# Later output projections one stage earlier, and the second group's operands inside the down-projections

## The chip, the cores and the metric

The kernel runs on one core of a Trainium2 chip. Its times are device microseconds of one launch; the profile adds one execution recorded by the hardware profiler. The engines are TensorE (PE for matmuls, PEld for weight loads), VectorE (DVE), ScalarE (ACT), GpSimd (POOL) and SyncE (SP), whose queue issues the transfers. Each runs its own instructions in a fixed order and waits on semaphores.

## The reference

One decoder layer for 2048 tokens of width 1024, in float32: a normalized and modulated input, attention beside a state-space mixer, an output projection, and a gated feed-forward of width 2816.

```python
mod = silu(c) @ w_ada + b_ada                       # shift1, scale1, gate1, shift2, scale2, gate2
h = modulate(rmsnorm(x, norm1_w), shift1, scale1)
q, k, v, z, xbc, dt_raw = split(h @ w_in)
attn = sliding_window_attention(rope(q), rope(k), v, sinks)      # window 128, 8 heads of 64
y = ssd_chunked_scan(silu(conv(xbc)), softplus(dt_raw), ...)     # chunks of 128, 8 heads of 64
y = grouped_rmsnorm(y * silu(z)) * ssm_norm_w
x = x + gate1 * (concat([attn, y]) @ w_out)
h = modulate(rmsnorm(x, norm2_w), shift2, scale2)
g, u = split(h @ w_gate_up)
x = x + gate2 * ((silu(g) * u) @ w_down)
return rmsnorm(x, final_norm_w)
```

## The kernel before

The 2048 tokens are four blocks of 512 (b = 0 to 3); two blocks make a group (s = 0, 1). Tiles have 128 partitions. Every float32 product is made of three passes (`mm3`, L269 to L271, or L876 to L878 in the feed-forward): each operand is split into a high and a low half, and high x high, high x low and low x high are added in PSUM. The splits are work of ACT (L807: the high half of a weight; L957: of an activation; L247: of a mixer output; L832 and L837: of a feed-forward operand) and of VectorE or GpSimd (L808, L802, L833: the low half). Split weights lie in a ring of six pairs (`w`), loaded weights in a ring of five (`raw`), passing values in a ring of eight (`t`), dense sums in four PSUM banks (`d`).

The stages follow each other on PE:
1. `opening()` (L1022): the modulation vectors (products with `w_ada`, L193 and L1052 on VectorE, and `ada_columns`, L173, through PE), the first norm of block 0, and the rotary tables `rope_tables` (L205, L207 to L223): for the sine and then the cosine, three operations (L214 to L216) round the angle, four (L219 to L222) reduce it, and ACT takes the sine (L223). `ready(d)` makes chunk d of the normalized input (L318, L320, L321); `whole(d)` also its modulation (two L1052). The rotary products are L369 and L370.
2. Input projections of the four blocks (`queries`, `keys_values`, `convolved`, `gated`), with the mixers (`attentions`, `ssds`) beside them.
3. `quads(0)` (L1254): gate and up projections of the first group as 22 `quad`s (L880) of seven half-size products each, in place of eight. Their operands are sums and differences of blocks: `operands_first` (L843), `operands_between` (L851), `operands_last` (L858). These load a block's residual from `mid` (L826), scale it by the root of the norm spread over partitions (L827; `at`, `am` and `bc` are that spread root), and split it into 28 pairs. The mixers of the last blocks run beside `quads(0)`.
4. `down(0)` and `down(1)` (L943): the down projections of blocks 0 and 1, in six groups g of the hidden width (five of four tiles, one of two), each with eight output chunks; L968 adds a PSUM sum to the residual and frees its bank. After a block, `final` writes the output: L997 on VectorE, L998 on SP. Beside them run `out_proj(2)` and `out_proj(3)` (L765; two halves for each of eight output chunks, weights by L257), whose 16 split inputs `mo` are loaded by `mixed` (L759), and the second group's operands.
5. `quads(1)`, `down(2)`, `down(3)`.

What sets the order: "beside" means that a main generator yields after each piece, and `tick(ratio)` adds `ratio` to a counter; whenever it reaches one, the first generator of the list `sides` makes a step. In stages 1 and 2 the instructions of PE (in the opening also of VectorE, SP and ACT) stand in the order in which the program writes them. In the rest a scheduler in the build orders each engine's instructions by its own model of their times. On the chip the orders are fixed.

`quad` also holds its first weight loads back: for the quad named `behind`, they are issued after the last load of `scaled`:

```python
with tc.issue_after(scaled.last.ins) if behind else nullcontext():
    a11, a21, a22, a12 = (load_w(wgu[f, u, half]) for u, half in ((0, 0), (1, 0), (1, 1), (0, 1)))
```

In the kernel before, `sides` beside `down(0)` holds `projections()`: both output projections and, beside the rest of the second, `operands_first` of the second group. Once that is done, within `down(1)`, the projections' pool is closed, the remaining operand tiles take its memory, and the remaining 20 of the 28 pairs are made beside the rest of `down(1)`.

## Time and profile before

| | us |
|---|---|
| median of 3 runs | 2442.17 |
| lowest, highest | 2438.68, 2443.37 |
| the profiled execution's own time | 2445.11 |
| its span | 2443.4 |
| PE busy, POOL busy, DVE busy, ACT busy | 2270.3, 1225.7, 1438.8, 969.1 |
| the first matmul of `down(0)` at | 1335.1 |
| the first matmul of `quads(1)` at | 1717.7 |

The granted clock of PE, averaged over the span, is 0.964. Times in the views count from the span's start. In a row of a timeline the first number is the start, the second the duration; what stands in brackets is the idle time of that engine before, and whose work ended it. PE's matmuls are pipelined, so its busy time is no measure of its peak; its idle pieces are what can be read.

### The profile page before, as it was taken

The page shows a single profiled execution, that of the slowest core. Times are in us where ns is not written, and L with a number is a line of the kernel's source. Part 1 is how long each engine was busy: PE and PEld are TensorE (multiplying, and loading weights), DVE is VectorE, ACT ScalarE, POOL GpSimd, SP SyncE. Part 2 cuts the span into 40 slices and gives each one's busy share as a digit, 9 for nine tenths or more (in the row PEclk, how much of TensorE's full clock was granted, in tenths as well). Part 3 has the DMA queues.
Part 4 walks back from the last instruction along what each step waited for, and adds up shares of the span by engine and source line. Part 5 has one row for each costly group of instructions (what it writes and reads, how often), then busy time and mean ns, then how long its engine had stood idle before and what let it go on. Part 6 is the DMA issues. An engine that isn't in the chain of part 4 may idle for free.

```text
span 2443.4 us, 33147 instructions
## 1 busy us (share of the span) xinstructions
PE 2270.3 (93%) x11304; PEld 1892.1 (77%) x11304; DVE 1438.8 (59%) x2543; ACT 969.1 (40%) x2011; POOL 1225.7 (50%) x1227
## 2 busy tenths in 40 slices
PE   6786999899899799999999999897799999999898
PEld 4676888789788688887887878686688888878687
DVE  5876874665366855576655534648854544444544
ACT  3454452555155545433334323223333333333332
POOL 1765533444124755587775224235766666643431
PEclk9898999999999899999999999899899999999998
DMA  6898978677775322233235665764422222263451
GB/s 243 275 336 282 315 241 260 218 242 241 261 266 173 125 82 73 75 117 96 86 95 183 195 194 163 239 199 143 163 85 76 95 78 78 82 215 104 136 166 52
DMA packets 249065, 412.22 MB, mean 169 GB/s; under 512 B 22464, under 2 KB 68544, under 8 KB 248896
## 3 DMA queue, kind: packets, MB, share of 16 engines
q1 hardware_dynamic: 247744, 409.05, 51.3%
q8 instruction: 89, 1.46, 0.2%
q10 hardware_dynamic: 1152, 1.05, 0.1%
q14 instruction: 80, 0.66, 0.1%
HBM read 315.58 MB, written 94.44 MB: 168 GB/s over the span
## 4 chain that ended last, share of the span: by engine, by line
PE 68%; DVE 11%; DMA 6%; POOL 5%; ACT 4%; issue 4%; SPq 1%; DVEq 0%; ACTq 0%; POOLq 0%
PE d L269 10%; PE d L271 10%; PE d L270 10%; PE d L878 7%; PE d L876 7%; PE d L877 7%; PE am L269 1%; PE am L270 1%; PE am L271 1%; PE am L878 1%; PE am L876 1%; PE am L877 1%; DMA t<-in_xT_dram 1%; DMA t<-mid 1%; DVE w L808 1%
## 5 line engine op out<-in xcount | busy, mean ns | idle before, releaser
L876 PE MATMUL d<-b,w 128*128 128x512 f32 x924 | 368.8, 403 | 31.6 <-ACT w L807 21.4
L807 ACT ACTIVATE w<-raw 128x512 fp32r<-128x512 f32 x316 | 198.2, 630 | 448.0 <-PE d L271 249.5
L878 PE MATMUL d<-b,w 128*128 128x512 f32 x924 | 368.6, 400 | 3.0 <-DVE w L808 3.0
L877 PE MATMUL d<-b,w 128*128 128x512 f32 x924 | 370.6, 401 | 0.6 <-POOL b L838 0.6
L269 PE MATMUL d<-a,w 128*128 128x512 f32 (+1 forms) x720 | 280.5, 399 | 16.1 <-ACT a L957 14.3
L270 PE MATMUL d<-a,w 128*128 128x512 f32 (+1 forms) x720 | 282.7, 394 | 0.1
L271 PE MATMUL d<-a,w 128*128 128x512 f32 (+1 forms) x720 | 282.6, 393 | 0.0
L808 POOL TENSOR_TENSOR w<-raw,w 128x512 fp32r<-128x512 f32 x88 | 119.0, 1353 | 278.7 <-ACT w L807 270.8
L808 DVE TENSOR_TENSOR w<-raw,w 128x512 fp32r<-128x512 f32 x228 | 210.2, 925 | 67.3 <-ACT w L807 65.9
L968 DVE SCALAR_TENSOR_TENSOR x<-d,mod,x 128x512 f32<-128x512 f32 (+1 forms) x182 | 131.1, 725 | 197.7 <-PE d L271 193.0
L876 PEld LDWEIGHTS d<-b,w 128*128 128x128 f32 x924 | 175.8, 190 | 73.2 <-ACT w L807 22.2
L269 PE MATMUL d<-w,hl 128*128 128x256 f32 (+1 forms) x608 | 181.9, 299 | 36.1 <-DVE s L370 16.6
L878 PEld LDWEIGHTS d<-b,w 128*128 128x128 f32 x924 | 175.7, 190 | 42.9 <-DVE w L808 4.2
L877 PEld LDWEIGHTS d<-b,w 128*128 128x128 f32 x924 | 176.1, 191 | 40.4 <-POOL b L838 1.3
L807 ACT ACTIVATE w<-s 128x512 fp32r<-128x512 f32 x176 | 111.0, 632 | 227.1 <-PE d L878 177.0
L808 POOL TENSOR_TENSOR w<-s,w 128x512 fp32r<-128x512 f32 x132 | 186.6, 1415 | 26.1 <-ACT w L807 25.7
L271 PE MATMUL d<-w,hl 128*128 128x256 f32 (+1 forms) x608 | 178.0, 293 | 2.1 <-DVE hl L321 2.1
L270 PE MATMUL d<-w,hl 128*128 128x256 f32 (+1 forms) x608 | 177.6, 292 | 0.0
L269 PEld LDWEIGHTS d<-a,w 128*128 128x128 f32 x720 | 137.4, 191 | 50.6 <-ACT a L957 17.0
L892 POOL TENSOR_TENSOR s<-raw,s 128x512 f32<-128x512 f32 x44 | 58.6, 1332 | 206.8 <-DVE w L808 125.0
L270 PEld LDWEIGHTS d<-a,w 128*128 128x128 f32 x720 | 137.4, 191 | 31.7 <-DVE a L802 1.0
L271 PEld LDWEIGHTS d<-a,w 128*128 128x128 f32 x720 | 137.3, 191 | 31.2
(356 smaller groups left out, 5476.4 us busy)
## 6 DMA issues: line engine op xcount, KB each, us to landing
raw<-in_wgu_dram SPq DMA_DIRECT2D x176, 256.0 KB, 2.8
raw<-in_wd_dram SPq DMA_DIRECT2D x176, 256.0 KB, 2.7
w<-w_x SPq DMA_DIRECT2D x48, 512.0 KB, 5.3
w<-w_o SPq DMA_DIRECT2D x48, 512.0 KB, 4.5
act<-t SPq DMA_DIRECT2D x88, 256.0 KB, 2.1
t<-act SPq DMA_DIRECT2D x88, 256.0 KB, 4.5
t<-in_xT_dram SPq DMA_DIRECT2D x80, 256.0 KB, 4.4
aw<-in_wada_dram SPq DMA_DIRECT2D x64, 256.0 KB, 4.3
```

The lines of the kernel that those rows point to most:

```text
L269: nc.tensor.matmul(out, ahi, bhi, start=first, stop=False)
L270: nc.tensor.matmul(out, ahi, blo, start=False, stop=False)
L271: mm3.last = nc.tensor.matmul(out, alo, bhi, start=False, stop=last)
L807: nc.scalar.activation(hi, x, AF.Copy)
L808: eng.tensor_tensor(lo, x, hi.bitcast(F32), ALU.subtract)
L876: nc.tensor.matmul(out, ahi, bhi, start=first and k == 0, stop=False, skip_group_check=True)
L877: nc.tensor.matmul(out, ahi, blo, start=False, stop=False, skip_group_check=True)
L878: mm3.last = nc.tensor.matmul(out, alo, bhi, start=False, stop=k == 3, skip_group_check=True)
L892: nc.gpsimd.tensor_tensor(s4, a12, s2, ALU.subtract)
L968: nc.vector.scalar_tensor_tensor(x, ps, gate2[:, c:c + 1], x, ALU.mult, ALU.add)
```

## The change

The multiset of instructions on each engine stays; their order changes.

- `RATIO_UP`, the pace of the mixers beside `quads(0)`, goes from 0.6 to 0.64. As soon as they are done, their memory is given back, and in it (a pool `op` on the right side) `first_output()` starts beside the rest of `quads(0)`: the loads of `mo` (a ring of 11 pairs, not 16) and `out_proj(2)`. What of it is left goes on beside `down(0)`.
- Beside `down(0)` follow `second_output()` (`out_proj(3)`) and `first_operands()`, at a pace of 0.55. When `sides` is empty, the pool `op` is closed, the remaining operand tiles take its place, and `last_operands()` (the 20 other pairs) runs beside `down(1)` at 0.3.
- Attention of blocks 1 to 3 waits no step (2 before) before its first tile.
- In the opening the sine's reduction is made before the first chunk (`next(tables)` before `ready(0)`), the cosine's after `ready(7)`, and ACT takes both sines at the end; the second set of modulation columns (`ada_columns`) comes before `whole(5)`.

Lines of the changed kernel stand four below those of the kernel before (L876 is L880, L826 is L830).

VectorE in the opening. Before, from the end of `ready(7)` to the first rotary products (L219 to L222 are the table's reduction, `aw` is `w_ada`):

```order
L219 SCALAR_TENSOR_TENSOR m_243<-m_242,m_240 128x512
L193 ISA aw,part<-aw,csil,vec 128x512
...
L220 SCALAR_TENSOR_TENSOR m_243<-m_242,m_243 128x512
...
L221 SCALAR_TENSOR_TENSOR m_243<-m_242,m_243 128x512
L222 TENSOR_SCALAR m_243<-m_243 128x512
L214 TENSOR_SCALAR m_665<-m_240 128x512
...
L219 SCALAR_TENSOR_TENSOR m_666<-m_665,m_240 128x512
...
L220 SCALAR_TENSOR_TENSOR m_666<-m_665,m_666 128x512
...
L221 SCALAR_TENSOR_TENSOR m_666<-m_665,m_666 128x512
L222 TENSOR_SCALAR m_666<-m_666 128x512
L369 TENSOR_TENSOR m_681<-d,cos 128x8x32
```

Now:

```order
L325 SCALAR_TENSOR_TENSOR hl_611<-t,mod,hl_611 128x512
L215 TENSOR_SCALAR m_664<-m_240 128x512
...
L216 TENSOR_SCALAR m_664<-m_664 128x512
...
L217 TENSOR_SCALAR m_664<-m_664 128x512
L220 SCALAR_TENSOR_TENSOR m_665<-m_664,m_240 128x512
...
L221 SCALAR_TENSOR_TENSOR m_665<-m_664,m_665 128x512
L222 SCALAR_TENSOR_TENSOR m_665<-m_664,m_665 128x512
...
L223 TENSOR_SCALAR m_665<-m_665 128x512
L373 TENSOR_TENSOR m_681<-d,cos 128x8x32
```

Only the cosine's seven operations are left between, and four L193 products in place of six (one L193 row is shown, in the first piece).

ScalarE at the end of the mixers in `quads(0)`. Before (L674 scales the mixer's last transposed output, `a` are the inputs of `down(0)`):

```order
L674 ACTIVATE m_13199<-st,vec 128x128 x4
L807 ACTIVATE w<-raw 128x512
L903 ACTIVATE t<-d 128x512
L907 ACTIVATE t<-d 128x512
L807 ACTIVATE w<-raw 128x512 x4
L930 ACTIVATE t<-t 128x512
L807 ACTIVATE w<-raw 128x512
L957 ACTIVATE a<-t 128x512 x4
L247 ACTIVATE mo<-t 128x512 x6
```

Now:

```order
L748 ACTIVATE m_12933,ss<-m_12866 128x256 x2
L811 ACTIVATE w<-s 128x512 x2
L755 ACTIVATE m_12866<-m_12866,rs 128x256 x2
L811 ACTIVATE w<-s 128x512
L678 ACTIVATE m_12933<-st,vec 128x128 x4
L251 ACTIVATE mo<-t 128x512 x6
L911 ACTIVATE t<-d 128x512
L251 ACTIVATE mo<-t 128x512 x2
```

The splits of `mo`, which stood behind the inputs of `down(0)`, follow the mixer's last scaling at once.

SyncE at the end of `down(1)`. Before:

```order
L826 DMA t<-mid_208 128x512
L813 DMA raw<-in_wd_dram 128x512
L826 DMA t<-mid_208 128x512 x2
L826 DMA t<-mid_207 128x512 x2
...
L813 DMA raw<-in_wgu_dram 128x512 x11
L998 DMA out_dram<-t 128x512
```

(the pair of rows with two loads each from `mid_208` and `mid_207` stands there four times). Now:

```order
L830 DMA t<-mid_208 128x512 x2
L830 DMA t<-mid_207 128x512
L817 DMA raw<-in_wd_dram 128x512
L830 DMA t<-mid_207 128x512
L817 DMA raw<-in_wd_dram 128x512 x2
L959 DMA t<-act_214 128x512 x2
L817 DMA raw<-in_wd_dram 128x512 x3
L817 DMA raw<-in_wgu_dram 128x512 x13
```

The last operand loads are now mixed with the loads of `w_down`, and the first loads of `w_gate_up` for `quads(1)` follow the last of these directly.

```diff
--- before.py
+++ after.py
@@ -29,7 +29,7 @@
 NEG = -1e30
 RAW, SPLIT = 5, 6
 TMP, M1, M2, M4 = 8, 3, 8, 4
-MIX, RATIO_UP = 1.1, 0.6
+MIX, RATIO_UP = 1.1, 0.64
 HALF = 32
 ROPE_THETA = 10000.0
 TWO_PI_1 = 6.25
@@ -209,6 +209,7 @@
         ang3 = ang.rearrange("p (t j) -> p t j", j=HALF)
         nc.vector.tensor_tensor(ang3, posf.unsqueeze(2).broadcast_to([P, S // P, HALF]),
                                 invf.unsqueeze(1).broadcast_to([P, S // P, HALF]), ALU.mult)
+        angles = []
         for dst, turn in ((sin, 0.0), (cos, 0.25)):
             k, r = common.m2(), common.m2()
             nc.vector.tensor_scalar(k, ang, 1.0 / (2 * math.pi), turn, ALU.mult, ALU.add)
@@ -220,6 +221,9 @@
             nc.vector.scalar_tensor_tensor(r, k, -TWO_PI_2, r, ALU.mult, ALU.add)
             nc.vector.scalar_tensor_tensor(r, k, -TWO_PI_3, r, ALU.mult, ALU.add)
             nc.vector.tensor_scalar(r, r, PI_IN, -PI_IN, ALU.min, ALU.max)
+            angles.append((dst, r))
+            yield
+        for dst, r in angles:
             nc.scalar.activation(dst.rearrange("p t j -> p (t j)"), r, AF.Sin)
         yield
 
@@ -535,7 +539,7 @@
             return q, kv
 
         held, nxt = None, load(0)
-        for _ in range(3 if b == 0 else 2):
+        for _ in range(3 if b == 0 else 0):
             yield
         for t in range(NT):
             gt, (q, kv) = b * NT + t, nxt
@@ -1084,6 +1088,7 @@
         ada_products(first, line, range(4, 8))
         reduced(0, rows0[1])
         scale_of(0)
+        next(tables)
         ready(0)
         weights(raws[0])
         main = queries(0, h)
@@ -1099,15 +1104,16 @@
         next(main)
         whole(4, rows4)
         weights(raws[2])
-        whole(5, rows5)
         line = side_bank(0)
         ada_products(second, line, range(8))
+        ada_columns(line, side_bank(0), 6)
+        whole(5, rows5)
         next(main)
-        ada_columns(line, side_bank(0), 6)
         weights(raws[3])
         ready(6)
         ready(7)
         next(main)
+        next(tables)
         drain(tables)
         return h, main
 
@@ -1255,63 +1261,70 @@
         for f in range(NF):
             yield from quad(s, f, ops, banks(f), f == 0, f == behind)
 
-    with tc.tile_pool(name="b0l", bufs=1, reuse_waits="tile") as bp:
-        operand_tiles(ops, bp, ("b22", "t3", "t2", "t4"))
-        main = quads(0, ops, lambda f: [dense() for _ in range(4)], 1)
-        next(main)
-        drain(operands_last(0, ops, bcs))
-        drain(beside(main, RATIO_UP))
-        finish(sides[-1] if sides else None)
+    bp = early.enter_context(tc.tile_pool(name="b0l", bufs=1, reuse_waits="tile"))
+    operand_tiles(ops, bp, ("b22", "t3", "t2", "t4"))
+    main = quads(0, ops, lambda f: [dense() for _ in range(4)], 1)
+    next(main)
+    drain(operands_last(0, ops, bcs))
+    for _ in beside(main, RATIO_UP):
+        if not sides:
+            break
+    finish(sides[-1] if sides else None)
+    mixing.close()
+    outputs = ExitStack()
+    op = outputs.enter_context(tc.tile_pool(name="op", bufs=1, side="right", reuse_waits="tile"))
+    mixes, ops = {2: [], 3: []}, {}
+
+    def output(b, each=lambda c: None):
+        yield from out_proj(b, y_of, mixes[b], lambda c: side_bank(c % 2), sums(op), lambda: side_bank(2), each)
+
+    def loaded(b, c):
+        mixed(b, mixes[b], (c,), lambda c: pair("mo", 11, pool=op))
+
+    def first_output():
+        for c in range(KT):
+            loaded(2, c)
+            if c % 2:
+                yield
+        yield from output(2, lambda c: loaded(3, c - 5) if c > 4 else None)
+
+    def second_output():
+        for c in range(3, KT):
+            loaded(3, c)
+            if c % 2:
+                yield
+        yield from output(3)
+
+    def first_operands():
+        bc = big("bc", 1, pool=op)
+        nc.scalar.copy(bc, spread(y_of[2], bc=side_bank(3)))
+        yield from operands_first(1, ops, [bc])
+
+    def last_operands():
+        bcs = [spread(y_of[2 + j], bc=side_bank(j)) for j in range(2)]
+        yield from operands_between(1, ops, bcs)
+        yield from operands_last(1, ops, bcs)
+
+    sides.append(first_output())
+    drain(beside(main, 0.5))
     early.close()
-    mixing.close()
-    dn = ctx.enter_context(tc.tile_pool(name="dn", bufs=1, side="right", reuse_waits="tile"))
-    with tc.tile_pool(name="b1", bufs=1, reuse_waits="tile") as bp:
-        ops = {}
+    dn = ctx.enter_context(tc.tile_pool(name="dn", bufs=1, reuse_waits="tile"))
+    with tc.tile_pool(name="b1", bufs=1, reuse_waits="tile") as bp, ExitStack() as late:
         operand_tiles(ops, bp, ("b11", "b21"))
-        with tc.tile_pool(name="op", bufs=1, reuse_waits="tile") as op:
-            mixes = {2: [], 3: []}
-
-            def outputs(b, each=lambda c: None):
-                yield from out_proj(b, y_of, mixes[b], lambda c: side_bank(c % 2), sums(op), lambda: side_bank(2), each)
-
-            def loaded(b, c):
-                mixed(b, mixes[b], (c,), lambda c: pair("mo", 16, pool=op))
-
-            def projections():
-                for c in range(KT):
-                    loaded(2, c)
-                    if c % 4 == 3:
-                        yield
-                yield from outputs(2, lambda c: loaded(3, c))
-                rest3 = outputs(3)
-                for _ in range(2):
-                    next(rest3)
-                    yield
-                bc = big("bc", 1, pool=op)
-                nc.scalar.copy(bc, spread(y_of[2], bc=side_bank(3)))
-                yield from both(rest3, operands_first(1, ops, [bc]))
-
-            sides.append(projections())
-            drain(beside(down(0, dn, dn), 0.42))
-            rest = down(1, dn, dn)
-            for _ in beside(rest, 0.8):
-                if not sides:
-                    break
-        with tc.tile_pool(name="b1l", bufs=1, reuse_waits="tile") as bp:
-            operand_tiles(ops, bp, ("t1", "b22", "t3", "t2", "t4"))
-            bcs = [spread(y_of[2 + j], bc=side_bank(j)) for j in range(2)]
-
-            def remaining():
-                yield from operands_between(1, ops, bcs)
-                yield from operands_last(1, ops, bcs)
-
-            sides.append(remaining())
-            last = sides[-1]
-            drain(beside(rest, 0.4))
-            finish(last)
-            for i, _ in enumerate(quads(1, ops, lambda f: [side_bank(i) if f % 2 else dense() for i in range(4)], 0)):
-                if i in (0, 2):
-                    norm_of_block_before(2)
+        sides.extend([second_output(), first_operands()])
+        last = None
+        for b in range(2):
+            for _ in beside(down(b, dn, dn), 0.3 if last else 0.55):
+                if not sides and last is None:
+                    outputs.close()
+                    bp = late.enter_context(tc.tile_pool(name="b1l", bufs=1, reuse_waits="tile"))
+                    operand_tiles(ops, bp, ("t1", "b22", "t3", "t2", "t4"))
+                    last = last_operands()
+                    sides.append(last)
+        finish(last)
+        for i, _ in enumerate(quads(1, ops, lambda f: [side_bank(i) if f % 2 else dense() for i in range(4)], 0)):
+            if i in (0, 2):
+                norm_of_block_before(2)
     drain(down(2, dn, dn))
     x3 = ctx.enter_context(tc.tile_pool(name="x3", bufs=1, reuse_waits="tile"))
     drain(down(3, dn, x3))
```

## The prediction

> **What bounds the kernel now.** I read the page first, then the table of waits of TensorE, then the windows by stage, then the timelines around the four longest waits.

> ```profile
> span 2443.4 us, 33147 instructions
> PE 2270.3 (93%) x11304; PEld 1892.1 (77%) x11304; DVE 1438.8 (59%) x2543; ACT 969.1 (40%) x2011; POOL 1225.7 (50%) x1227
> ```

> PE is busy 93% of the span and no other engine reaches 60%. The change gives every engine the same instructions as before, in another order. So PE's 2270 us can only shrink where they ran at half clock; what can move otherwise is the 173 us in which PE waits. The waits are few and named:

> ```profile
> PE d L876 <- ACT w L807: 21.4, 1, 21.4
> PE d L269 <- DVE s L370: 16.6, 2, 16.3
> PE d L269 <- ACT a L957: 14.3, 6, 3.2
> PE am L269 <- DMA w<-w_o: 8.3, 1, 8.3
> PE d L878 <- DVE w L808: 3.0, 2, 2.5
> PE st L313 <- DVE t L311: 3.9, 2, 2.1
> ```

> The columns are the total, the number of times and the longest. The first, second and fourth rows, 46 us in three waits, all lie where the change works. By stage (us, then busy time of PE, PEld, DVE, ACT, POOL, then PE's granted clock):

> ```profile
> 1335.00:1520.00 185.00, 181.81 (x770) 146.71 (x771) 83.18 (x108) 60.72 (x101) 65.15 (x48) 0.98 0.61 198
> 1520.00:1600.00 80.00, 69.92 (x289) 55.36 (x288) 45.77 (x86) 20.52 (x34) 18.60 (x14) 0.91 0.68 218
> 1600.00:1660.00 60.00, 60.00 (x265) 48.75 (x264) 31.49 (x53) 17.93 (x30) 21.29 (x16) 1.00 0.61 194
> 1660.00:1722.00 62.00, 40.13 (x162) 31.08 (x161) 54.96 (x68) 24.69 (x42) 40.09 (x28) 0.81 0.45 142
> 1722.00:1760.00 38.00, 33.35 (x130) 25.48 (x130) 35.32 (x41) 10.98 (x19) 29.72 (x22) 0.91 0.51 170
> ```

> The first row is most of `down(0)`, the second the hand-over from `down(0)` to `down(1)`, then `down(1)` in two pieces, then the start of `quads(1)`. PE is full in the first and third (60 us hold 265 matmuls, 0.226 us each); in the fourth VectorE is busy 55 of 62 us and PE waits. The work that makes VectorE late there was waiting to start while VectorE idled half of 1335 to 1660. That unevenness is what the change rearranges.

> **The opening** (PE waits 16.3 us for the first rotary products, which need both tables).

> ```profile
> 24.11 0.75 DVE L318 SCALAR_TENSOR_TENSOR t<-m,scl,at 128x512 f32<-128x512 f32 x1 [3.01 <-PE at L313]
> 69.90 0.68 DVE L219 SCALAR_TENSOR_TENSOR m<-m,m 128x512 f32<-128x512 f32 x1
> 81.78 1.75 DVE L193 CUSTOM_DVE_ANT_0 aw<-aw,csil,vec 128x512 f32<-128x512 f32 x1
> 85.12 0.74 DVE L193 CUSTOM_DVE_ANT_0 aw<-aw,csil,part 128x512 f32<-128x512 f32 x1
> 87.56 0.43 DVE L222 TENSOR_SCALAR m<-m 128x512 f32<-128x512 f32 x1
> 88.68 0.42 DVE L369 TENSOR_TENSOR m<-d,cos 128x256 f32<-128x256 f32 x1 [0.70 <-ACT cos L223]
> ```

> After the last normalized chunk VectorE runs eleven table operations and six L193 products from 69.90 to 87.99, 18.1 us, and only then the rotary products. The sine half (four operations: two neighbours of the first and last, 0.68, 0.68, 0.68, 0.43) now fits into an idle piece of 3.0 us that ended at 24.11; two L193 products (1.75 and 0.74) fall behind the rotary products. Removed: 2.5 + 2.5 = 5.0 us. What stays, seven table operations and four products, costs between 7 us (each at its short duration, 0.43, 0.68 or 0.74) and 13.1 us (18.1 less 5.0, with the long ones as they were). So the gain is 5 to 11, nearer 5 since what stretched the products there is not touched; against it stand the column sums of the modulation, which now precede chunk 5 and delay that chunk, covered by key/value matmuls already mixed in. **I take 6.5 us**, ends 3 and 10.

> **The end of `quads(0)`.** The mixers now end about 100 matmuls sooner (`RATIO_UP` 0.64), and eleven of the sixteen half-chunks of `out_proj(2)` fill the tail. Two prices. First, the last mixer's chain on PE, ACT and GpSimd:

> ```profile
> 1297.10 1.03 PE L716 MATMUL st<-state,m 128*128 128x256 f32 x4
> 1312.65 0.91 ACT L751 ACTIVATE m<-m,rs 128x256 f32<-128x256 f32 x2 [1.12 <-POOL rs L238]
> 1317.10 1.14 ACT L674 ACTIVATE m<-st,vec 128x128 f32<-128x128 f32 x4 [0.26 <-PE st L671]
> ```

> From L716 to the end of L751 it took 16.5 us. Before, PE had other work until the transposes L671; now only 55 matmuls (12.5 us at 0.226) stand between, so PE waits about 3 us at the transposes. Then ACT must do the four L674 scalings (1.14 us) and the first splits of `mo` before `out_proj(2)` can start, since they are queued behind those scalings and it follows the transposes at once: about 2 us more. Such a gap also costs clock:

> ```profile
> 1335.00:1339.00 4.00, 3.89 (x12) 0.70 1.02 364
> 1335.11 1.19 PE L269 MATMUL d<-a,w 128*128 128x512 f32 x4 [2.27 <-ACT a L957]
> ```

> The gap of 2.27 us at the start of `down(0)` was followed by a granted clock of 0.70 over 4 us, 1.2 us lost. So **+6 us**, ends 0 (VectorE and GpSimd run the chain uncontended and the splits are early) and 10. [...] Second, the `w_o` loads. They precede their matmuls by 26 to 56 matmuls, 6 to 13 us, and the page has

> ```profile
> w<-w_o SPq DMA_DIRECT2D x48, 512.0 KB, 4.5
> 1549.37 0.84 SPq L257 DMA_DIRECT2D w<-w_o  x1
> 1556.65 0.79 PE L269 MATMUL am<-mo,w 128*128 128x512 f32 x1 [8.27 <-DMA w<-w_o]
> ```

> 4.5 us to landing in the median, against the 7.2 us of the one load (issued at 1549.37, PE released at 1556.6) that held PE for 8.3 us. The tightest would then be 1 us late: nothing taken, end +3. `down(0)` itself loses `out_proj(2)` and keeps a VectorE that is busy 83 of 185 us: nothing.

> **The hand-over.** Row two of the stages: 10.1 us idle, and 80 x 0.09 = 7.2 us of clock, 17.3 us in all. The `w_o` wait goes, since those loads now stand 40 matmuls ahead. What is left is a burst on SP's queue: loads of the residual and of the activations stand behind eight output stores that wait for VectorE's L997, and I read two waits of PE from the order, about 3 and 3.5 us, each with 1.2 of clock: 8.9. **Gain 8 us**, ends 2 and 13.

> **The second group's operands in `down(1)`.** This is the 21.4 us.

> ```profile
> 1674.55 38.83 SPq L826 DMA_DIRECT2D t<-mid  x16
> 1713.72 2.23 SPq L813 DMA_DIRECT2D raw<-in_wgu_dram  x5
> 1717.70 0.79 PE L876 MATMUL d<-b,w 128*128 128x512 f32 x1 [21.36 <-ACT w L807]
> ```

> The releaser named, ACT, is only the last link: SP stood 38.8 us with sixteen loads that waited for buffers that VectorE had to free, the gate and up weights are queued behind them, arrived from 1713.72 on, and PE started 4 us later. In the change all 28 steps of the operands run inside `down(1)` and the weight loads are queued before its end, so this queue is gone. Its price is that 432 matmuls of `down(1)` (98 us at 0.226) now carry 146 VectorE instructions. Their durations in this stretch of the run before:

> ```profile
> L968 DVE SCALAR_TENSOR_TENSOR x<-d,mod,x 128x512 f32<-128x512 f32 x48 | 35.5, 747 | 48.8 <-PE d L271 44.2 <-DMA x<-mid 4.6
> L808 DVE TENSOR_TENSOR w<-raw,w 128x512 fp32r<-128x512 f32 x26 | 22.9, 882 | 0.7 <-ACT w L807 0.7
> L833 DVE SCALAR_TENSOR_TENSOR b<-t,mod,b 128x512 fp32r<-128x512 f32 x12 | 12.8, 1073 | 0.1
> L802 DVE TENSOR_TENSOR a<-t,a 128x512 fp32r<-128x512 f32 x9 | 10.3, 1141 | 8.4 <-ACT a L957 8.3
> L827 DVE SCALAR_TENSOR_TENSOR t<-t,scl,at 128x512 f32<-128x512 f32 x12 | 8.7, 736 | 0.1
> L827 DVE SCALAR_TENSOR_TENSOR t<-t,scl,bc 128x512 f32<-128x512 f32 x8 | 7.9, 1008 | 6.7 <-DMA t<-mid 6.7
> L867 DVE SCALAR_TENSOR_TENSOR t<-t,mod 128x512 f32<-128x512 f32 x4 | 5.2, 1289 | 0.0
> L808 DVE TENSOR_TENSOR w<-raw,w 128x512 fp32r<-128x512 f32 x18 | 12.9, 717 | 0.0
> ```

> 39 x 0.747 + 17 x 0.882 + 12 x 1.073 + 9 x 1.141 + 24 x 0.736 + 8 x 1.008 + 8 x 1.289 (L867 and its like L865) = 103; the 29 small ones left, at about 0.45, make 13: 116 us. That is 18 us more than PE's 98. The last row is L808 in a quieter stretch (2180 to 2280): 717 ns instead of 882. If all that swing shrink so (a fifth to a third on L808, L833, L802 and L867), the sum is 102, 4 us over. So VectorE is overbooked by 4 to 18 us, a little of it hidden by four accumulator banks; GpSimd will be busy some 60 of the 98 us, nearer the crowded case. I take **13 us of waits in place of 21.4**, in many small pieces, with VectorE as the bound; the half clock around the hole (0.81 over 62 us is mostly the idle piece itself) is worth another 1.5. **Gain 10 us**, ends 2 and 19. [...]

> **The start of `quads(1)`.** The waits of 2.5 (L878) and 2.1 us (L313) came with a VectorE busy 35 of 38 us and a clock of 0.91 (3.4 us lost). With operands and weights ready before, one wait for the root of `norm_of_block_before` stays, about 3 us. **Gain 4 us**, ends 0 and 6.

> **The middle.** Attention of the later blocks starts two steps sooner beside the projections (the `0` in place of `2`), which shifts every later mixer step by two. The stages before `quads(0)`:

> ```profile
> 250.00:800.00 550.00, 518.53 (x3216) 463.10 (x3215) 334.44 (x841) 265.90 (x653) 207.34 (x326) 0.98 0.74 244
> 800.00:1335.00 535.00, 517.71 (x2489) 426.67 (x2487) 336.56 (x501) 233.85 (x532) 363.47 (x353) 0.98 0.32 100
> ```

> PE idles 31 us in the first row, in waits of 1 to 6 us; they are dealt anew. **0 us**, ends -8 and +8, nothing in the trace decides the sign.

> **Sum.** -6.5 + 6 - 8 - 10 - 4 + 0 = -22.5 on the profiled execution's 2445.1 (span 2443.4 and 1.7 around it): 2422.6. The median of the runs, 2442.2, lies 2.9 under that execution: **2420 us**, 0.9% less. Ends together, as independent (3.5, 5, 5.5, 8.5, 3, 8, and 3 for the loads): about 15 either way, 2405 to 2435.

> **Rivals.**
> - *VectorE is not the bound in `down(1)`* (quiet durations, four banks hide the rest): the 13 us vanish, 2407. For it speaks the 717 row, against it the 40 us of GpSimd in 62.
> - *The gains are real but eaten in the middle*: attention brought forward meets keys or values not ready, and 8 us of new waits there, with 16 in place of 6 at the end of `quads(0)`, leave about 2438, no change. For it: L957's six waits and the small waits of that part show that every hand-over costs 2 to 4 us.
> - *The projections choke the tail of `quads(0)`; slower.* `out_proj(2)` takes its weights through the six split buffers that the quad products use, and SP issues in order; if a landing takes 10 us there, two of 4.5 us behind each other, the eight half-chunks with the shorter leads wait 3 + 1.2 us each, 34 us, and the time is 2454. It decides from landings of about 8 us on. For it: the 7.2 us load at the hand-over. Against: the share of the transfer engines in 800 to 1335 (0.32) is half of that at the hand-over (0.68), and the loads lead by 6 to 13 us.
> - *The change does not do what it says*, and the operands still end after `down(1)`: the order shows the weight loads behind the last operand load and before the last matmuls of `down(1)`, so the 21.4 us could only come back if VectorE ran 20 us late; 2430.

> **Chances.** The forecast 0.55 (2405 to 2435), VectorE not the bound 0.19, eaten in the middle 0.1, choked tail 0.1, operands late 0.06. A measurement of this kernel cannot tell less than 0.2%, 5 us, from no change. The first, second and last are faster, but for 0.01 of the first; of the third 0.08 is no change and 0.02 slower. Faster 0.79, same 0.09, slower 0.12. For 8 in 10 the range goes from 2400 to 2443.

> **What would show it.** Right: no wait above 5 us at the first L876 of `quads(1)`; PE waiting in `down(1)` for L968's release in pieces of 1 to 3 us, VectorE over 90% busy there; no `w_o` wait of 8 us; the first rotary product at about 82; a new wait of 3 to 5 us at the last L671 or the first `am` matmul. Wrong: PE waits for `w_o` in the tail of `quads(0)`; SP standing with loads from `mid` and the gate weights behind them; or new waits of over 8 us together between 250 and 830.

## The result and the profile after

The changed kernel takes 2411.3 us in the median (2408.7 to 2414.8), the kernel before 2442.6: a ratio of 0.9876 with a 95% interval of 0.9862 to 0.9889, or 30 us less. The forecast was 2420 us, with 2400 to 2443 as its range. The page of the changed kernel:

```profile
span 2407.0 us, 33175 instructions
PE 2267.8 (94%) x11304; PEld 1887.6 (78%) x11304; DVE 1445.4 (60%) x2543; ACT 966.2 (40%) x2011; POOL 1230.1 (51%) x1227
```

The busy times are those of before within 7 us; what went is waiting. Of the waits of TensorE these answer to the rows shown before:

```profile
PE d L273 <- ACT a L961: 12.2, 5, 3.0
PE d L273 <- DVE x L972: 9.9, 8, 2.8
PE d L273 <- ACT t L282: 7.7, 1, 7.7
PE am L273 <- DMA w<-w_o: 2.8, 1, 2.8
PE am L273 <- ACT mo L251: 1.8, 1, 1.8
PE am L274 <- DVE mo L252: 1.2, 1, 1.2
```

The waits of 21.4, 16.3 and 8.3 us are gone. In their places stand eight small ones for L972 (L968 before) with 9.9 us together (the first, 2.8 us, at the hand-over, the others in `down(1)`), one of 7.7 us in the opening, one of 2.8 us for `w_o`, and a new pair of 1.8 and 1.2 us where `out_proj(2)` starts beside `quads(0)`. By stage (us, then busy time of PE, PEld, DVE, ACT, POOL, then the granted clock):

```profile
1500.00:1560.00 60.00, 57.08 (x248) 45.54 (x247) 26.38 (x44) 17.99 (x30) 27.20 (x20) 1.00 0.55 180
1560.00:1660.00 100.00, 87.91 (x358) 67.78 (x357) 95.34 (x136) 40.26 (x68) 48.98 (x33) 0.97 0.72 239
1581.00:1692.00 111.00, 103.19 (x420) 79.94 (x419) 106.88 (x134) 49.02 (x85) 67.74 (x46) 0.97 0.56 180
1692.00:1745.00 53.00, 52.22 (x226) 41.17 (x225) 30.91 (x49) 16.28 (x28) 37.06 (x28) 1.00 0.42 144
```

The third row is `down(1)` whole, the fourth the start of `quads(1)`. VectorE is busy 107 of 111 us in `down(1)` and PE waits 8 us there; then `quads(1)` starts without a wait and at full clock. SyncE's queue at that place:

```profile
1662.01 7.25 SPq L817 DMA_DIRECT2D raw<-in_wd_dram  x3
1669.36 19.02 SPq L817 DMA_DIRECT2D raw<-in_wgu_dram  x8
```

The gate and up weights are issued from 1669.4 on, 22 us ahead of the first matmul of `quads(1)` at 1691.6; before, the first was issued 4 us ahead.

To set the two profiled executions against each other, here is the time that PE lost in each stage: for every matmul, the time to the start of the next beyond what that shape takes in its fast fifth, summed. The stages are cut at the same counts of matmuls, so where pieces were moved from one stage to the other the cut is rough. The last three columns belong to experiments below.

| lost time, us | before | change | staging alone | pace alone | best |
|---|---|---|---|---|---|
| opening | 30.4 | 24.0 | 29.2 | 29.6 | 23.7 |
| projections and mixers, to the first `quad`s | 149.5 | 146.4 | 145.3 | 154.2 | 146.0 |
| `quads(0)` with its end | 39.5 | 42.1 | 46.4 | 41.2 | 41.0 |
| `down(0)` | 6.8 | 3.9 | 8.7 | 2.2 | 2.4 |
| hand-over | 16.2 | 10.7 | 11.3 | 10.5 | 9.7 |
| `down(1)` | 25.3 | 15.1 | 15.9 | 11.6 | 10.8 |
| start of `quads(1)` | 10.4 | 2.6 | 2.7 | 2.4 | 2.3 |
| the rest | 31.9 | 31.2 | 33.1 | 31.9 | 31.0 |
| sum | 310.0 | 276.0 | 292.6 | 283.6 | 266.9 |

The change loses 34 us less. Its profiled execution is one of the faster (2408.7, the median is 2411.3) and that of before one of the slower, so 36 us of span stand for 30 us between the kernels. Since the same matmuls run in both, the sums ought to differ by those 36 us, so the measure is good to about 2 us.

One row needs more care. Up to 1270 us, late in `quads(0)`, the engines execute the same instructions in the same order in "before", "staging alone" and "pace alone", and yet the second row has 149.5, 145.3 and 154.2 us there. A difference of less than some 5 us in that row, between single executions, says nothing.

### The profile page after: what moved, and what is told of

Read it like the earlier page. It is cut to its first block, busy times and chain, and to the rows that moved or that the text cites. A ratio compares the mean times of both kernels' runs of the same rounds, so it can differ in the third digit from the quotient of the medians.

```text
span 2407.0 us, 33175 instructions
## 1 busy us (share of the span) xinstructions
PE 2267.8 (94%) x11304; PEld 1887.6 (78%) x11304; DVE 1445.4 (60%) x2543; ACT 966.2 (40%) x2011; POOL 1230.1 (51%) x1227
## 4 chain that ended last, share of the span: by engine, by line
PE 67%; DVE 12%; DMA 7%; POOL 5%; issue 5%; ACT 3%; SPq 1%; DVEq 0%; POOLq 0%; ACTq 0%
PE d L273 9%; PE d L275 9%; PE d L274 9%; PE d L881 7%; PE d L880 7%; PE d L882 7%; DMA t<-in_xT_dram 2%; PE am L273 1%; PE am L274 1%; PE am L275 1%; PE am L880 1%; DMA t<-act 1%; PE am L882 1%; PE am L881 1%; DMA t<-mid 1%
## 5 line engine op out<-in xcount | busy, mean ns | idle before, releaser
L880 PE MATMUL d<-b,w 128*128 128x512 f32 x924 | 366.2, 400 | 12.0 <-ACT b L841 9.2
L812 DVE TENSOR_TENSOR w<-raw,w 128x512 fp32r<-128x512 f32 x228 | 213.1, 937 | 72.8 <-ACT w L811 72.1
L812 POOL TENSOR_TENSOR w<-raw,w 128x512 fp32r<-128x512 f32 x88 | 119.9, 1363 | 247.3 <-ACT w L811 228.4
L972 DVE SCALAR_TENSOR_TENSOR x<-d,mod,x 128x512 f32<-128x512 f32 (+1 forms) x182 | 130.7, 724 | 162.5 <-PE d L275 159.8
L880 PEld LDWEIGHTS d<-b,w 128*128 128x128 f32 x924 | 174.7, 189 | 53.5 <-ACT b L841 11.8
L812 POOL TENSOR_TENSOR w<-s,w 128x512 fp32r<-128x512 f32 x132 | 188.2, 1428 | 30.6 <-ACT w L811 29.6
L273 PEld LDWEIGHTS d<-a,w 128*128 128x128 f32 x720 | 137.0, 191 | 60.6 <-ACT a L961 15.1
## 6 DMA issues: line engine op xcount, KB each, us to landing
w<-w_x SPq DMA_DIRECT2D x48, 512.0 KB, 5.3
w<-w_o SPq DMA_DIRECT2D x48, 512.0 KB, 4.7
```

What stands on the lines that cost most here:

```text
L273: nc.tensor.matmul(out, ahi, bhi, start=first, stop=False)
L812: eng.tensor_tensor(lo, x, hi.bitcast(F32), ALU.subtract)
L880: nc.tensor.matmul(out, ahi, bhi, start=first and k == 0, stop=False, skip_group_check=True)
L972: nc.vector.scalar_tensor_tensor(x, ps, gate2[:, c:c + 1], x, ALU.mult, ALU.add)
```

## The experiments

Each kernel was timed against the kernel before on the same chip, in five rounds. Interval means the 95% interval of the ratio.

### The opening alone

```diff
+        next(tables)
         ready(0)
...
-        whole(5, rows5)
         line = side_bank(0)
         ada_products(second, line, range(8))
-        next(main)
         ada_columns(line, side_bank(0), 6)
+        whole(5, rows5)
+        next(main)
         weights(raws[3])
         ready(6)
         ready(7)
         next(main)
+        next(tables)
         drain(tables)
```

(with `rope_tables` as in the change, on the kernel before)

> The kernel before with only the opening of the change (sine reduction ahead of the first chunk, cosine after the last, both sines together, modulation columns one chunk earlier). Theory (the opening's gain is its own and is kept): first rotary product at 83 to 84 us in place of 90.25, the end 5 to 7 us earlier, ratio about 0.9975. Rival (PE only reaches its next wait, on the key/value side and the first attention, sooner): the rotary product moves, the end by less than 2 us, ratio 0.999 to 1.001. Nothing else changes, the wait of 21.4 us stays.

Measured: 0.9982, interval 0.9971 to 0.9993. The waits:

```profile
PE d L880 <- ACT w L811: 20.8, 1, 20.8
PE d L273 <- ACT t L282: 6.5, 1, 6.5
```

The product that waited 16.3 us now waits 6.5 and starts at 83.2 in place of 90.2; the hole of 21 us stays. The stage's lost time falls by 7.1 us (30.4 to 23.3); the interval of the ratio is 1.7 to 7.1 us, 4.4 in the middle. So the gain is the opening's own and real. Whether some of it is given back in the next waits is not shown: the projections lose 2.4 us more here, which is less than that row varies between executions of the same order.

### Earlier attention alone

```diff
-        for _ in range(3 if b == 0 else 2):
+        for _ in range(3 if b == 0 else 0):
```

> The kernel before with only the earlier attention (0 in place of 2 steps). Theory: waits between 395 and 830 are dealt anew and the sum is about -3 us, ratio 0.9985 to 0.9995, within what cannot be told from none. Rival (it is a real gain of its own): -6 us or more, ratio below 0.9976; other rival: slower by up to 4 us, the gain of the middle in the change came from elsewhere.

Measured: 0.9980, interval 0.9971 to 0.9989, about -5 us. The interval is 2.7 to 7.1 us: the gain is real, and it excludes neither the 3 us expected nor the 6 of the rival. Lost time in the projections and mixers falls from 149.5 to 142.6 us. One pair of executions would not show that, but all fourteen profiled ones agree: by this measure the row has 144 to 154 us, 149 in the mean, in the five kernels that wait two steps, and 140 to 146, 144 in the mean, in the nine that wait none.

### The staging alone

The change without its opening and without the earlier attention: the pace 0.64, the projections beside the end of `quads(0)`, the operands in `down(1)`.

```diff
-        for _ in range(3 if b == 0 else 0):
+        for _ in range(3 if b == 0 else 2):
```

(on the changed kernel, with `opening` and `rope_tables` of the kernel before)

> The change without its opening and without the earlier attention: only the pace 0.64, the projections beside the end of quads(0), and the operands inside down(1). Theory: the staging carries about 22 to 25 us of the 31 (hand-over, operands, start of quads(1)), ratio 0.990 to 0.991, with the small waits for L972 in down(1) as in the change. Rival (the gain is shared about equally with the middle and the opening): below 18 us, ratio above 0.9925.

Measured: 0.9948, interval 0.9933 to 0.9963: 13 us, against 22 to 25 expected. The rival's number, but not its reason. The hole is gone as in the change (start of `quads(1)`: 2.7 us lost); what is missing lies at the end of `quads(0)`, in timeline rows of PE:

```profile
1301.78 1.12 PE L671 MATMUL st<-ident,m 128*128 128x128 f32 x4 [5.46 <-ACT m L751]
1304.64 0.80 PE L269 MATMUL am<-mo,w 128*128 128x512 f32 x1 [1.75 <-ACT mo L247]
```

and in two waits of the norm's matmuls for the sum of squares that GpSimd adds up:

```profile
PE sm L284 <- POOL acc L279: 8.5, 2, 5.2
```

The first fence is the double wait that the prediction put there (about 3 and 2 us; here 5.5 and 1.75), the second was in no term. GpSimd itself was not late there: before its last addition, at 1586.70, it stood idle for 1.84 us, waiting for a square from ScalarE, which waited for VectorE, which had stood 1.9, 1.2 and 0.9 us for loads of the residual at the hand-over. A like wait is followed row by row below, under the pace of 0.72.

### Staging with earlier attention

The changed kernel with only the opening taken back.

> The change without its opening: earlier attention and the staging together. Staging alone gave 0.9948 and attention alone 0.998, the whole 0.9876. Theory (the two steps of attention decide where the last mixer's chain falls at the end of quads(0), so that the new wait there shrinks): the wait at the last L671 is about 2 us in place of 5.5, the wait for the first mo split stays about 1.2 to 1.8, and the ratio is 0.989 to 0.991, that is more than the product 0.9928. Rival (the missing part comes with the opening): ratio 0.992 to 0.994, the wait at L671 stays 5 us.

Measured: 0.9892, interval 0.9875 to 0.9908. The waits:

```profile
PE st L671 <- ACT m L751: 2.6, 1, 2.6
PE am L269 <- ACT mo L247: 1.8, 1, 1.8
```

The one wait of 2.6 us left for L751 lies at 390 us in the changed kernel too; at the end of `quads(0)` it is gone, and so are the waits for the sums of squares. So these two parts do not add: staging alone gives 13 us, attention alone 5, both 26. The two steps of attention move the last mixer's chain away from the place where PE waits for it at the end of `quads(0)`: with the staging alone PE has 4.7 us of other work between the mixer's last state matmul (L716) and the transposes that need the chain, and the chain takes 10.5; with both, PE has 14.0 us and the chain takes 13.0. Why the sums of squares come in time here was not tried; from the first place where these kernels differ, the scheduler makes the order anew in each.

### One number: the pace beside `down(0)`

```diff
-            drain(beside(down(0, dn, dn), 0.42))
+            drain(beside(down(0, dn, dn), 0.62))
```

> The kernel before with one number changed: the pace of the projections beside down(0) 0.62 in place of 0.42, so that they end sooner and the second group's operands start sooner in down(1); nothing is moved into quads(0) and the ring mo keeps 16 pairs. Theory (the hole of 21.4 us is operands that start too late; spreading them is what counts): the hole falls below 5 us, VectorE over 90% busy in most of down(1) with several waits of PE for L968, and most of the staging's gain is there: 15 to 22 us, ratio 0.991 to 0.994. Rival (the projections must leave down(0) for quads(0), else VectorE and SP are late at the hand-over instead): the hole shrinks but the hand-over grows, gain below 8 us, ratio above 0.9967.

Measured: 0.9893, interval 0.9875 to 0.9911: 26 us, more than expected, from one number and without moving anything into `quads(0)`. In the table its column has what the staging gains at the hand-over, in `down(1)` and at the start of `quads(1)`, and none of what that costs at the end of `quads(0)`. (Its profiled execution is the slowest of its five; the 154.2 us of the second row are no cost of the pace, since that code comes in the same order as before.) Windows of `down(0)` and of the stretch in which `down(1)` begins:

```profile
1335.00:1520.00 185.00, 181.37 (x780) 146.61 (x779) 86.05 (x126) 59.91 (x98) 55.40 (x42) 0.99 0.65 213
1560.00:1660.00 100.00, 93.52 (x400) 73.69 (x399) 72.07 (x105) 34.44 (x58) 46.55 (x34) 1.00 0.75 250
```

VectorE does no more in `down(0)` than before (86 us against 83), but in 1560 to 1660 it is busy 72 us where it was 52 before: the second group's operands start while it has time.

### The hold on the first weight loads

```diff
-            for i, _ in enumerate(quads(1, ops, lambda f: [side_bank(i) if f % 2 else dense() for i in range(4)], 0)):
+            for i, _ in enumerate(quads(1, ops, lambda f: [side_bank(i) if f % 2 else dense() for i in range(4)], -1)):
```

> The kernel before, with the first gate and up loads of quads(1) no longer held behind the last operand load; in SyncE's order seven of them now stand ahead of the last 20 operand loads. Theory (the hole of 21.4 us is VectorE finishing the operands late; the queue is only the last link): the first matmul of quads(1) comes up to 21 us sooner, but PE then waits in the first quad for the operands it needs next, and all waits of down(1) and the start of quads(1) together fall by 6 us at most; ratio 0.9975 to 1.000. Rival (the queue is the cause): the hole goes and does not come back, 15 to 20 us, ratio 0.992 to 0.994.

Measured: 0.9944, interval 0.9929 to 0.9959. Lost time of `down(1)` and of the start of `quads(1)` together falls from 35.7 to 24.5 us, between the theory's 6 and the rival's 15 to 20. PE now reaches `quads(1)` without a wait and then stands in the first `quad`; the two longest waits there, in rows of its timeline:

```profile
1700.52 0.80 PE L876 MATMUL d<-b,w 128*128 128x512 f32 x1 [5.06 <-ACT b L837]
1710.15 0.80 PE L876 MATMUL d<-b,w 128*128 128x512 f32 x1 [2.89 <-ACT b L837]
```

So the hole had two causes of about the same size: weight loads queued behind the operand loads (11 us), and operands late on VectorE (14 us of waits for `b` that come instead). That makes 11 of the 14 us; the interval is 10 to 17, and up to 1674 us, near the end of `down(1)`, all instructions come in the same order as before.

### Is VectorE the bound in `down(1)`? Two ways

Ten low halves of weights to GpSimd:

```diff
-halves(load_w(wd4[g, c]), nc.gpsimd if c % 2 else nc.vector)
+halves(load_w(wd4[g, c]), nc.gpsimd if c % 2 or b == 1 and c % 4 else nc.vector)
```

> The change with ten of the low halves of weights in down(1) moved from VectorE to GpSimd (three of four chunks there in place of two). By the mean of this row before (0.88 us) that takes 9 us of work from VectorE in down(1). Theory (VectorE is the bound between the hand-over and quads(1), the waits of PE for L972 are its lateness): those waits, 9.9 us in the change, fall by 4 us or more and the run is 4 to 8 us below the change's, ratio to before about 0.985. Rival (the waits come from loads that arrive in a burst at the hand-over, VectorE is busy only because it stalls on them and on GpSimd): no change within 2 us, or slower, since GpSimd takes 1.35 us for what VectorE does in 0.9.

Measured: 0.9885, interval 0.9867 to 0.9902, as the change. The waits for L972 fall from 9.9 to 7.9 us, and a new one comes:

```profile
PE d L273 <- DVE x L972: 7.9, 7, 2.4
PE sm L288 <- POOL acc L283: 4.7, 1, 4.7
```

That left it open: VectorE's part of the waits fell by 2 us, and a wait of 4.7 us came at the hand-over. (GpSimd, which the row names, was idle for 1.3 us before that addition; it waited for a square whose operand, the input `xT`, was loaded behind the output stores.) So, twenty low halves not computed at all:

```diff
+        if eng is None:
+            nc.scalar.activation(lo, x, AF.Copy)
...
-halves(load_w(wd4[g, c]), nc.gpsimd if c % 2 else nc.vector)
+halves(load_w(wd4[g, c]), nc.gpsimd if c % 2 else None if b == 1 else nc.vector)
```

> The change, with twenty low halves of weights in down(1) not computed: the low half is a second copy of the high one, made by ScalarE, so block 1 of the output is not the layer's. That takes 18 to 20 us of work from VectorE there (20 x 0.9 to 1.0), gives GpSimd none and ScalarE 12.6 us (20 x 0.63). Theory (VectorE's work bounds down(1)): the waits of PE for L972, 9.9 us in the change, fall below 3 us, and waits of down(1) as a whole by 8 us or more; the run 7 to 12 us below the change's, ratio 0.983 to 0.985. Rival (it is the burst at the hand-over and the order, as the move to GpSimd left it open): L972 stays above 6 us, ratio 0.987 to 0.989.

Measured: 0.9872, interval 0.9855 to 0.9888. The run says rival, the stage says theory in part:

```profile
1581.00:1685.00 104.00, 99.95 (x419) 79.33 (x418) 92.01 (x119) 56.43 (x98) 66.26 (x47) 0.98 0.62 189
PE d L273 <- DVE x L975: 6.9, 4, 2.8
PE d L273 <- ACT a L964: 18.2, 5, 8.5
```

(first row a window, then waits; L975 is L972 of the change, L964 is L961). VectorE has 15 us less to do in `down(1)`, and the stage takes 104 us in place of 111, 7 us less. The waits for L975 in it fall from 7.1 to 4.0 us; the first one, 2.9 us, and one of 2.3 us for activations stay, but they lie ahead of the stage, at the hand-over. Most of the 7 us is given back early in `down(3)`, where the wait for activations is 8.5 us in place of 2.8, in a part that the edit does not touch. SyncE's order differs there: five output stores and a load of weights stand ahead of the first of those activations, in the change three stores; the load is issued 30.4 us after `down(3)` began in place of 26.2, and it lands 4.3 us later in place of 2.8. So taking 15 of VectorE's 107 us away removes about half of the 15 us lost in `down(1)`. What the other half is, this run does not show: VectorE is still busy 92 of 104 us, so more of it may be VectorE's load too.

### More pace, less pace, and both ideas together

Four kernels around these. Three are the kernel before with the change's opening and attention, nothing moved into `quads(0)`, and a pace beside `down(0)` of 0.62, 0.72 and 0.56; the last is the change with 0.62 in place of its 0.55.

```diff
-            drain(beside(down(0, dn, dn), 0.42))
+            drain(beside(down(0, dn, dn), 0.62))
```

> The kernel before with the pace 0.62 beside down(0), the change's opening and its earlier attention, nothing moved into quads(0). Theory (the parts add: -27 by the pace, -3 by the opening, -4 by attention): 2405 to 2409 us on the scale of 2440, ratio 0.986, some 3 us below the change's ratio of 0.9876. Rival (parts do not add, since each shift deals the middle's waits anew): 0.988 to 0.991, no better than the pace alone.

Measured: 2401.4 us, 0.9839, interval 0.9824 to 0.9855. It beats the kernel before by 39 us, and the change too, whose interval begins at 0.9862. Here the parts do add: 26, 4 and 5 us alone, 39 together (interval 35 to 43). Its lost time is the last column of the table. A wait for L972 of 5.2 us in two pieces is what is left of VectorE's lateness, and `down(1)` has 16 us less of VectorE's work than in the change (window of 105 us):

```profile
PE d L273 <- DVE x L972: 5.2, 2, 2.9
1579.00:1684.00 105.00, 99.69 (x417) 79.39 (x416) 90.92 (x125) 43.99 (x76) 68.04 (x47) 0.97 0.59 183
```

With 0.72:

> As the one with pace 0.62, with 0.72. Theory (spreading VectorE's work over more of down(0) and down(1) takes more of the waits for L968 away): waits of PE in down(1) 3 us or more below those at 0.62 and the run 2 to 5 us faster. Rival (at 0.62 the rest is the hand-over and not VectorE's load; a higher pace crowds the loads of the projections' weights in down(0)): equal or slower.

Measured: 0.9888, interval 0.9872 to 0.9903. The waits for L972 shrink from 5.2 to 3.6 us, less than the theory had, and another takes their place, in rows of its waits:

```profile
PE d L273 <- ACT a L961: 15.1, 8, 3.2
PE sm L288 <- POOL acc L283: 11.5, 2, 8.2
```

The row names GpSimd, but GpSimd is only the last link. The wait of 8.2 us, followed back row by row:

```profile
1581.90 1.26 POOL L283 TENSOR_TENSOR acc<-acc,t 128x512 f32<-128x512 f32 x1 [2.94 <-ACT t L282]
1581.13 0.63 ACT L282 ACTIVATE t<-t 128x512 f32<-128x512 f32 x1 [3.51 <-DVE t L782]
1580.34 0.75 DVE L782 SCALAR_TENSOR_TENSOR t<-at,mod,t 128x512 f32<-128x512 f32 x1 [2.60 <-DMA t<-in_xT_dram]
1574.77 0.43 SPq L781 DMA_DIRECT2D t<-in_xT_dram  x1
```

GpSimd, ScalarE and VectorE each stood idle, for 2.9, 3.5 and 2.6 us, and what they waited for is the input `xT` of the last output chunk, which SyncE issues behind the output stores, residual loads and weight loads of the hand-over and which lands 5.6 us later. So it is the hand-over's queue again, as the first half of the rival had it.

With 0.56:

> The kernel before with the change's opening and attention, as the one with pace 0.62 (0.9839), with 0.56. Theory (what counts is that the last operand loads stand ahead of the last weight loads of down(1); at 0.56 four of them come directly ahead of the gate weights): no hole above 5 us at the start of quads(1), more lateness of VectorE late in down(1) than at 0.62, ratio 0.984 to 0.988. Rival (the hole returns below some pace as a whole): a wait of 10 us or more at the first matmul of quads(1), ratio above 0.990.

Measured: 0.9916, interval 0.9899 to 0.9932. Neither the one nor the other: no hole of 10 us, but waits of 2.8, 1.0 and 3.7 us at the start of `quads(1)` and 7.5 us for `w_o`, and its runs spread over 13 us. The queue is not what makes the first of these waits:

```profile
1669.45 2.97 SPq L817 DMA_DIRECT2D raw<-in_wgu_dram  x5
1683.93 1.71 POOL L890 TENSOR_TENSOR s<-raw 128x512 f32<-128x512 f32 x1
1686.36 0.50 PE L880 MATMUL d<-b,w 128*128 128x512 f32 x1 [2.81 <-ACT w L811]
```

The gate weights are issued 13 us ahead of the first matmul of `quads(1)` at 1682.8. The split that PE waits for needs a sum of two weights, and GpSimd, which stands at the additions of `down(1)`'s squares until 1684, makes it only then.

So 0.56, 0.62 and 0.72 give 20, 39 and 27 us. Each number makes another order, and what differs are single waits, for `w_o`, for `xT`, for a sum of weights. 0.62 is the best of three tried; that it lies near an optimum is not shown.

The change with 0.62:

> The change with its pace beside the down projections 0.62 in place of 0.55: the projections that start in quads(0) stay there, the operands start sooner in down(1). The kernel with the old place of the projections and 0.62 gave 0.9839. Theory (moving projections into quads(0) buys nothing once the operands start in time, and costs its own wait for the mo split): waits of VectorE in down(1) shrink by 2 to 5 us, the 3 us at the start of out_proj(2) stay, ratio 0.985 to 0.987, not below 0.9839. Rival (both gains add): ratio 0.981 to 0.983.

Measured: 0.9956, interval 0.9943 to 0.9968. Both sides missed: 17 us slower than the change with 0.55 by the medians. The start of `out_proj(2)` waits as expected (1.8 and 1.2 us), but 15 us more are lost at the hand-over and 6 us more in `down(1)`. SyncE and VectorE there:

```profile
1566.32 1.65 SPq L1002 DMA_DIRECT2D out_dram<-t  x3
1569.50 0.49 SPq L953 DMA_DIRECT2D x<-mid  x1
1576.71 3.67 SPq L959 DMA_DIRECT2D t<-act  x4
1573.97 0.75 DVE L972 SCALAR_TENSOR_TENSOR x<-d,mod,x 128x512 f32<-128x512 f32 x1 [1.68 <-DMA x<-mid]
1576.59 0.75 DVE L972 SCALAR_TENSOR_TENSOR x<-d,mod,x 128x512 f32<-128x512 f32 x1 [1.87 <-DMA x<-mid]
```

VectorE itself waits for the residual `x`, whose loads are issued between and behind the output stores of block 0; the loads of the next activations come after them. That is the queue that the prediction described at the hand-over, and with more operand loads put into the same stretch the stage loses 25 us in place of 11. (5.5 us of it lie earlier, at 1544, in a wait for activations that are issued ahead of the stores.) The order of the queue is not all of it. In the next rows, of the change and of this run, the last two numbers are the busy share of the transfer engines and what they moved in GB/s:

```profile
1562.00:1578.00 16.00, 10.96 (x49) 8.11 (x48) 12.35 (x26) 5.08 (x9) 4.65 (x4) 1.00 1.00 348
1566.00:1586.00 20.00, 10.98 (x30) 6.85 (x28) 14.97 (x25) 5.70 (x10) 3.08 (x2) 0.77 0.96 334
```

At the hand-over the transfer engines are full (busy 1.00 and 0.96 of these stretches), so another order alone can here only choose what comes late. The same number is best in one arrangement and bad in the other.

## Why the prediction was right, and where not

The direction was right, and the time lies within the range; the gain is a third larger than forecast: 22 us were forecast between the medians, 30 were measured (on the profiled execution -22.5, and 34 us less were lost there). The time alone would not decide for this mechanism: 2411 lies nearer to the 2407 of the rival without VectorE's bound than to 2420. Term by term, by the table of lost time:

- **Opening**, forecast -6.5: measured -6.4 by the stage (30.4 to 24.0). The count of what stays between the last chunk and the rotary products held: VectorE starts them at 81.94, forecast 82, in the row

```profile
81.94 0.42 DVE L373 TENSOR_TENSOR m<-d,cos 128x256 f32<-128x256 f32 x1 [0.70 <-ACT cos L227]
```

- **End of `quads(0)`**, forecast +6: measured +2.6. The mechanism was right, and with the staging alone it shows in full, 5.5 and 1.75 us and +6.9 in that stage. In the change the first of the two waits is gone, because the earlier attention moves the last mixer's chain. The failed step is the chain "16.5 us against 55 matmuls": it took the mixers' place in `quads(0)` from the order, but their instructions on ACT and GpSimd at the speed and in the company of before. In the changed kernel the chain from L720 (L716 before) to the end of L755 takes 13.1 us, and PE reaches the transposes 14.0 us after L720.
- **`down(0)`**, forecast nothing: -2.9. A wait of 3.1 us for activations at 1465 does not come. That `out_proj(2)` is mostly out of this stage is not the reason: the pace alone, with `out_proj(2)` in it, loses 2.2 us there, and the staging alone 8.7.
- **Hand-over**, forecast -8: -5.5. What failed is the step by which 40 matmuls of lead remove the wait for `w_o`. The wait for `w_o` did not go but shrank to 2.8 us; of the two others, forecast as 3 and 3.5, the trace has 2.8 (L972) and 2.2 us (L961).
- **Operands in `down(1)`**, forecast -10: -10.2. Right on the place, the engine and the row (L972): VectorE is busy 107 us in a stage of 111 (forecast 116 us of work against 98 of PE's), and the waits come in pieces, of which this is the longest:

```profile
1650.94 0.77 PE L273 MATMUL d<-a,w 128*128 128x512 f32 x1 [2.70 <-DVE x L972]
```

  That the size fits is partly luck. The forecast set 13 us of waits in place of the hole of 21.4; PE's idle time in the stage is 7.8 us. The other 7 of the 15 us lost are matmuls that start late or run slow, 3.4 of them in 6.8 us at half clock behind the row above. By the run without twenty low halves, taking 15 us of VectorE's work away removes about half of the 15 us; the rest stays open. Two of the durations moved as well, with GpSimd busy 61% of the stage against 46% in the stretch from which they were taken: L812 takes 1.10 us where 0.88 was used, but L837 0.89 where it was 1.07:

```profile
L812 DVE TENSOR_TENSOR w<-raw,w 128x512 fp32r<-128x512 f32 x17 | 18.7, 1101 | 0.4 <-ACT w L811 0.4
L837 DVE SCALAR_TENSOR_TENSOR b<-t,mod,b 128x512 fp32r<-128x512 f32 x12 | 10.5, 885 | 0.2
```

- **Start of `quads(1)`**, forecast -4: -7.8. The mis-sized term. A wait of 3 us for the root of the norm was left standing; it did not come, and of the 10.4 us lost there before, the forecast had counted 8 (waits of 2.5 and 2.1 us, and 3.4 of clock). The four kernels of the table without the hole lose 2.3 to 2.7 us there.
- **Middle**, forecast 0: -3.1, which is within what this row varies with the same code. Attention alone gave about 5 us by the times, interval 3 to 7. "Nothing in the trace decides the sign" was fair, and a gain of about 5 us was left out.

The sum of the misses is -11 us, of which the median keeps 8 or 9 (2420 against 2411). The largest are the start of `quads(1)`, where the hole's after-effects were mis-sized, the mixers' chain, which the attention moved, and the middle, which was taken as nothing.

Of the rivals, the choked tail did not come, nor did new waits in the middle that eat the gain, nor operands that end after `down(1)`. The quiet case (no VectorE lateness) did not come either, though its time is near: VectorE is busy 96% of `down(1)`, and PE waits for L972 there. What no term asked is whether the projections had to move at all. The pace alone gives 26 of the 30 us: the hole came from operands that started late and from the weight loads queued behind them, and starting them sooner by one number removes both. The forecast's own reading ("the work that makes VectorE late there was waiting to start while VectorE idled") already said so.

What stays open: what makes the other half of the 15 us lost in `down(1)`, and how much of the differences between these kernels is the order that the scheduler happens to make. No run here held that order fixed while one cause was changed. The waits at the hand-over and early in `down(3)` that name GpSimd or ScalarE lead back, where they were followed, to SyncE's order of stores and loads.

## What to carry to other kernels

When a stage ends in a long wait whose releaser is a short chain (loads, split, matmul), look at the queue ahead of the loads and at the engine that frees their buffers, and then back along that engine for the stretch where it idled: starting the work sooner by one pace number may be worth as much as moving stages. Parts of a rescheduling need not add: staging, attention and opening gave 13, 5 and 4 us alone and 30 together, while pace, attention and opening gave 26, 5 and 4 alone and 39 together. So a part should be tried with and without the others before it is judged. Follow a wait back link by link: the engine that a row names may itself have been idle, and here three such waits ended at one queue. At the hand-over, where the transfer engines were busy 0.96 to 1.00 of the time (stores, residual loads, activations on one queue), more work in the same stretch made what stood behind it late: 25 us lost in place of 11. And compare a stage's profile with that of a kernel that has the same order there before a difference is called a gain: here it moved by up to 9 us between them.

## What the runs showed of the hardware

```profile
1506.74:1510.16 3.42, 1.72 (x8) 1.08 (x6) 0.75 (x1) 0.41 (x1) 1.28 (x1) 1.00 0.80 243
1646.71:1650.12 3.41, 1.53 (x7) 0.91 (x5) 3.41 (x4) 1.15 (x2) 3.41 (x3) 1.00 0.74 251
1650.16:1653.57 3.41, 2.62 (x6) 2.15 (x7) 3.41 (x6) 1.24 (x2) 1.87 (x2) 0.50 0.71 226
```

PE idles 1.70 us of the first and 1.88 us of the second, and only the second is followed by half clock. With both traces cut into stretches of that length at the changes of clock, 44 stretches at full clock were followed by half clock, and all but one of these had over 1.6 us of idle time; 1272 were followed by full clock, and none of these had more than 1.75. So in these two traces a gap costs clock when about half of one such stretch is idle, and whether a gap of 2 to 3 us does that depends on where it falls.
